# GpSimd in place of SP waits for the last store, and each store has a semaphore of its own

## The chip, the cores and the metric

The kernel runs on one core of a Trainium2 chip. The metric is the device time of one execution in microseconds (us); the median of the runs is given, with the lowest and highest. The core has five engines that run their own instruction streams and meet through semaphores: TensorE (PE), VectorE (DVE), ScalarE (ACT), GpSimd (POOL, or Pool) and SyncE (SP). SP computes nothing; here it issues transfers and waits.

## What is computed

The reference multiplies 16 pairs of matrices, the second one transposed:

```python
batch, m, k, n = 16, 512, 512, 512
a: (batch, m, k) float32
b: (batch, n, k) float32
out = np.matmul(a, b.transpose(0, 2, 1)).astype(np.float32)
```

## The kernel before

**Work and tiles.** The 16 batch elements are taken in 8 pairs. A load brings one input for a whole pair, 2 MB, so there are 16 loads, alternately of `a` and `b`, into the seven slots of `ld`. DVE casts each load to bf16 in two halves of k (`ha`, `wa` for a; `hb`, `wb` for b), PE transposes them in 128x128 blocks into PSUM (`tp`), ACT and DVE copy the results to `ta` and `tb`, PE multiplies them into `ps`, and ACT copies each 512x512 result into one of the seven slots of `ob`. Each result leaves as one store of 1 MB: 16 stores. PE, DVE and ACT run this in loops of the chip over the 8 pairs (L149, L185, L224).

**Who issues and who waits.** The order of the transfers is written out by hand. SP issues all loads (L96) and, between them, tells DVE of each landed load (L116). The string `STORES` (L33) is Pool's list: its eight S are the stores 0 to 7, issued by Pool when ACT has filled the slot (L108, L109); its nine O are waits for the stores 0 to 8 to land, each of which gives a slot of `ob` back to ACT (L135). The stores 8 to 15 are issued by SP, six of them at the places that `LATE` (L36) names and the last two behind all loads. Behind them SP waits for the stores 9 to 14 (L125). Store 15, the last, is waited for in a second critical section (L266, L267). The engines that wait are told apart by `nc.sync` (SP) and `nc.gpsimd` (Pool).

**Semaphores.** A transfer adds 16 to its semaphore when all of it has landed. `landed(n)` (L98) gives the semaphore and the value that stand for store n. Before, Pool's eight stores share five semaphores (`SW = 5`), and a wait for a second store on the same one waits for 32; SP's stores use the semaphores of the load slots, whose count goes on from what the loads have left there:

```python
if n < STORES.count("S"):
    return s_st[n % SW], 16 * (n // SW + 1)
slot = (n - STORES.count("S") + 2) % NL
return s_ld[slot], 16 * (len(range(slot, 2 * pairs, NL)) + 1 + (n - STORES.count("S") >= NL))
```

**The end of the program.** Both critical sections are `tc.tile_critical(no_gpsimd_drain=True)`: with that, the framework puts a NOP on Pool, and a drain on the other engines, behind a section. Between the sections SP collects a signal from each engine (L44). Behind the wait of the second section the engine that waited signals once more (L266). At the end of the whole context, all under L293, every engine has a drain, Pool gathers their signals and releases them, Pool clears the range of semaphores that the program used (EVENT_SEMAPHORE_RANGE_CLEAR), and a second barrier of the same kind closes. In the built program before, Pool's stream behind its L135 waits is: the NOP of L44, the first drain of L293, the gathering of the first barrier, a second drain, the clear, a third drain and the second barrier. SP's is: the signals of L44, a NOP of L266, the waits of L293 (the wait of L267 is among them), a branch, the signal, drain and NOP of L266, and two drains of L293. The cleared range is 99 to 132.

Of the kernel before, what the change touches and what calls it, by code (L numbers as in the profile page):

```python
# [10 lines left out]
def kernel(  # L11
# [6 lines left out]
    nc = tc.nc  # L18
    P = 128
    batch, M, K = a.shape  # L20
# [5 lines left out]
    pairs = batch // 2  # L26
    f32 = mybir.dt.float32
    bf16 = mybir.dt.bfloat16
    NL = 7
# [1 line left out]


    STORES = "SSSSOSOSOSSOOOOOO"  # L33
    SW = 5

    LATE = {11: (8, 9), 13: (10, 11), 15: (12, 13)}  # L36

# [3 lines left out]
    def sem(name):  # L41
        return tc.alloc_semaphore(name)

    with tc.tile_critical(no_gpsimd_drain=True):  # L44
# [11 lines left out]

        s_set = sem("s_set")
        s_ld = [sem(f"s_ld{i}") for i in range(NL)]
        s_st = [sem(f"s_st{i}") for i in range(SW)]

        s_go = sem("s_go")
        s_of = sem("s_of")
# [33 lines left out]
            nc.sync.dma_start(ld[:, slot], src).then_inc(s_ld[slot], 16)  # L96

        def landed(n):  # L98

            if n < STORES.count("S"):  # L100
                return s_st[n % SW], 16 * (n // SW + 1)

            slot = (n - STORES.count("S") + 2) % NL
            return s_ld[slot], 16 * (len(range(slot, 2 * pairs, NL)) + 1 + (n - STORES.count("S") >= NL))

        def store(n):
            engine = nc.gpsimd if n < STORES.count("S") else nc.sync
            engine.wait_ge(s_out, n + 1)  # L108
            engine.dma_start(  # L109
                out[n].rearrange("(p j) n -> p j n", j=J), ob[:, n % NO]  # L110
            ).then_inc(landed(n)[0], 16)

        for n in range(NL):
            load(n)
        for n in range(2 * pairs):
            nc.sync.wait_ge(s_ld[n % NL], 16 * (n // NL + 1)).then_inc(s_go, 1)  # L116

            if n > 0 and n + NL - 1 < 2 * pairs:
                load(n + NL - 1)
            for m in LATE.get(n, ()):  # L120
                store(m)
        store(batch - 2)
        store(batch - 1)
        for n in range(batch - NO, batch - 1):
            nc.sync.wait_ge(*landed(n))  # L125
# [4 lines left out]
        for what in STORES:  # L130
            if what == "S":
                store(n_st)
                n_st += 1
            else:
                nc.gpsimd.wait_ge(*landed(n_of)).then_inc(s_of, 1)  # L135
                n_of += 1
# [127 lines left out]


    with tc.tile_critical(no_gpsimd_drain=True):  # L266
        nc.sync.wait_ge(*landed(batch - 1))  # L267


# [28 lines left out]
```

## Time and profile before

| | us |
|---|---|
| median of 3 runs (lowest, highest) | 125.75 (125.67, 125.76) |
| the profiled execution | 125.76 |
| its span, first to last instruction of the program | 124.0 |
| busy: PE, DVE, ACT, POOL | 92.2, 68.2, 68.1, 5.8 |
| moved in all, mean rate over the span | 50.33 MB, 406 GB/s |
| last store issued by SP (L109) | 114.42 |
| waits of SP at L125 start, first and last | 115.3, 120.2 |
| branch of SP behind the wait for store 15 (L293) | 122.7 |

Times inside the execution count from the start of the span. Busy time is of engine instructions only: semaphore, branch, drain and transfer-issuing instructions belong to an engine's queue and are marked with a q (SPq, POOLq). They are not in the busy figures, but the profile lists them by line with their number, their shortest, median and longest duration in ns, and the first and last start. Line 293 is the launch line at which the context closes; instructions that the framework adds there are recorded under it, even where their wait is written elsewhere.

### The profile page before, as it was taken

The page shows a single profiled execution, that of the slowest core. Times are in us where ns is not written, and L with a number is a line of the kernel's source. Part 1 is how long each engine was busy: PE and PEld are TensorE (multiplying, and loading weights), DVE is VectorE, ACT ScalarE, POOL GpSimd, SP SyncE. Part 2 cuts the span into 40 slices and gives each one's busy share as a digit, 9 for nine tenths or more (in the row PEclk, how much of TensorE's full clock was granted, in tenths as well). Part 3 has the DMA queues.
Part 4 walks back from the last instruction along what each step waited for, and adds up shares of the span by engine and source line. Part 5 has one row for each costly group of instructions (what it writes and reads, how often), then busy time and mean ns, then how long its engine had stood idle before and what let it go on. Part 6 is the DMA issues. An engine that isn't in the chain of part 4 may idle for free. (4 is left out here: it accounts for less than half of the span.)

```text
span 124.0 us, 2364 instructions
## 1 busy us (share of the span) xinstructions
PE 92.2 (74%) x768; PEld 57.5 (46%) x768; DVE 68.2 (55%) x96; ACT 68.1 (55%) x130; POOL 5.8 (5%) x14
## 2 busy tenths in 40 slices
PE   0005099998999899999989998996699909996000
PEld 0005097457547744764476467444554509542000
DVE  0006595948891898389568668913967059400000
ACT  4002415669558946885595679536756085566000
POOL 2000000000000070002020200000000000000000
PEclk9999999999999999999999999999999995999975
DMA  5899999999999999999999999999999999999980
GB/s 100 360 434 444 434 428 423 428 423 423 434 434 434 428 428 407 449 410 441 426 423 441 412 447 428 418 428 428 436 442 410 423 428 426 423 428 426 428 349 11
DMA packets 4608, 50.33 MB, mean 406 GB/s; under 512 B 512, under 2 KB 512, under 8 KB 512
## 3 DMA queue, kind: packets, MB, share of 16 engines
q1 hardware_dynamic: 3456, 41.94, 80.2%
q0 software_dynamic: 1152, 8.39, 16.0%
HBM read 33.55 MB, written 16.78 MB: 406 GB/s over the span
## 5 line engine op out<-in xcount | busy, mean ns | idle before, releaser
L253 PE MATMUL ps<-tb,ta 128*128 128x512 bf16 x256 | 57.7, 379 | 0.4
L211 ACT COPY ob<-ps 128x512 f32 x64 | 34.4, 589 | 29.5 <-PE ps L253 23.2
L193 ACT COPY ta<-tp 128x512 bf16<-128x512 bf16 x64 | 33.0, 610 | 15.7 <-PE tp L234 15.7
L253 PEld LDWEIGHTS ps<-tb,ta 128*128 128x128 bf16 x256 | 24.1, 98 | 30.5 <-issue 3.9
L234 PE MATMUL tp<-ident,ha 128*128 128x128 bf16 x256 | 20.0, 235 | 13.8 <-PEq L139 13.8
L234 PEld LDWEIGHTS tp<-ident,ha 128*128 128x128 bf16 x256 | 17.2, 106 | 17.2 <-issue 15.3
L234 PE MATMUL tp<-ident,hb 128*128 128x128 bf16 x256 | 19.1, 234 | 7.3 <-PEq L139 7.1
L174 DVE COPY tb<-tp 128x1024 bf16<-128x1024 bf16 x32 | 21.2, 684 | 4.8 <-DVEq L139 4.8
L234 PEld LDWEIGHTS tp<-ident,hb 128*128 128x128 bf16 x256 | 17.0, 106 | 8.0 <-issue 8.0
L158 DVE CAST hb<-ld 128x1024 bf16 x8 | 5.5, 688 | 12.7 <-DVEq L139 12.7
L169 DVE COPY ha<-wa 128x2048 bf16<-128x2048 bf16 x8 | 5.5, 690 | 11.4 <-DVEq L139 11.4
L158 DVE CAST ha<-ld 128x1024 bf16 x8 | 5.5, 687 | 10.1 <-DVEq L139 10.0
L164 DVE CAST wa<-ld 128x2048 bf16 x8 | 9.7, 1218 | 0.0
L164 DVE CAST wb<-ld 128x2048 bf16 x8 | 9.7, 1216 | 0.0
L109 POOL DMA_DIRECT2D out_dram<-ob x8 | 5.1, 644 | 64.8 <-DMA ld<-in_b_dram 41.4
L173 DVE COPY hb<-wb 128x2048 bf16<-128x2048 bf16 x8 | 5.5, 685 | 0.2
L161 DVE CAST ha<-ld 128x1024 bf16 x8 | 5.5, 688 | 0.0
L161 DVE CAST hb<-ld 128x1024 bf16 x8 | 5.5, 685 | 0.0
L184 ACT ACT_TABLE_LOAD x1 | 1.3, 1283 | 1.1 <-SPq L44 1.1
L80 POOL TENSOR_SCALAR_AFFINE_SELECT ident<-ident 128x128 bf16<-128x128 bf16 x1 | 0.3, 282 | 0.2 <-POOL ident L78 0.2
L78 POOL MEMSET ident<- 128x128 bf16 x1 | 0.2, 204 | 0.5 <-SPq L44 0.5
L184 ACT COPY one<-const-float32-1.0 128x1 f32<-128x1 f32 x1 | 0.2, 191 | 0.0
(4 smaller groups left out, 0.4 us busy)
## 6 DMA issues: line engine op xcount, KB each, us to landing
ld<-in_a_dram SPq DMA_DIRECT2D x8, 2048.0 KB, 27.8
ld<-in_b_dram SPq DMA_DIRECT2D x8, 2048.0 KB, 30.3
out_dram<-ob POOLq DMA_DIRECT2D x8, 1024.0 KB, 28.7
out_dram<-ob SPq DMA_DIRECT2D x8, 1024.0 KB, 20.4
```

The costliest lines, as they stand in the source:

```text
L109: engine.dma_start(out[n].rearrange("(p j) n -> p j n", j=J), ob[:, n % NO]).then_inc(landed(n)[0], 16)
L158: nc.vector.tensor_copy(out=h[:, :J, :], in_=src[:, :J, :HK]).then_inc(s_cd, 1)
L161: nc.vector.tensor_copy(out=h[:, J:, :], in_=src[:, J:, :HK]).then_inc(s_c, 1)
L164: nc.vector.tensor_copy(out=w[:], in_=src[:, :, HK:]).then_inc(s_w, 1)
L169: nc.vector.tensor_copy(out=ha[:], in_=wa[:]).then_inc(s_ca, 1)
L173: nc.vector.tensor_copy(out=hb[:], in_=wb[:]).then_inc(s_cb, 1)
L174: nc.vector.tensor_copy(out=tb[:, ko, :], in_=tp[:, 2 + ko % 2].rearrange("k j p -> k (j p)"),).then_inc(s_eb, 1)
L184: nc.scalar.copy(out=one[:], in_=nc.const_aps.tensor(1.0, (P, 1), f32))
L193: c = nc.scalar.copy(out=ta[:, ko, e * J * P:(e + 1) * J * P].rearrange("k (j p h) -> k j p h", j=J, h=2), in_=tp[:, ko % 2, :, e * HP:(e ...
L211: c = nc.scalar.copy(out=dst[:, j, :].rearrange("m (p j) -> m p j", j=2 * J), in_=ps[:, j, :].rearrange("m (j p) -> m p j", j=2 * J),)
L234: t = nc.tensor.transpose(tp[:, 2 * x + g, j, :], h[:, j, g * P:(g + 1) * P], ident[:])
L253: t = nc.tensor.matmul(ps[:, j, :], ta[:, ko, (e * J + j) * P:(e * J + j + 1) * P], tb[:, ko, :].rearrange("k (j p) -> k j p", j=2 * J)[:, ...
```

## The change

The wait for store 15 in the second critical section goes from SP to Pool, and each of the 16 stores gets a semaphore of its own, waited for at 16. The helper `landed` becomes one line.

```diff
-    SW = 5
...
-        s_st = [sem(f"s_st{i}") for i in range(SW)]
+        s_st = [sem(f"s_st{i}") for i in range(batch)]
...
         def landed(n):
-            if n < STORES.count("S"):
-                return s_st[n % SW], 16 * (n // SW + 1)
-            slot = (n - STORES.count("S") + 2) % NL
-            return s_ld[slot], 16 * (len(range(slot, 2 * pairs, NL)) + 1 + (n - STORES.count("S") >= NL))
+            return s_st[n], 16

         def store(n):
             engine = nc.gpsimd if n < STORES.count("S") else nc.sync
             engine.wait_ge(s_out, n + 1)
             engine.dma_start(
                 out[n].rearrange("(p j) n -> p j n", j=J), ob[:, n % NO]
-            ).then_inc(landed(n)[0], 16)
+            ).then_inc(s_st[n], 16)
...
     with tc.tile_critical(no_gpsimd_drain=True):
-        nc.sync.wait_ge(*landed(batch - 1))
+        nc.gpsimd.wait_ge(*landed(batch - 1))
```

The kernel's own semaphores go from 28 to 39, and the framework takes one more (a signal of Pool), so that the cleared range becomes 99 to 144. In the built program after, the streams of PE, DVE and ACT are as before but for line numbers, six lower, and so are the issues and waits of SP and Pool up to the end of the first section. The NOP, the waits and the branch, then the signal and the NOPs of the second section now stand on Pool, ahead of its first drain of the closing (L287 is what was L293, L260 what was L266). SP has in their place a wait for Pool's signal, ahead of its two drains.

## The prediction

> **What bounds the kernel now.** I read the page's span and slices first: 124.0 us of span, with the DMA row full until the last two slices, so everything ahead of the last store is set by transfers. Then I cut the end of the span into three stretches with the table by windows (bounds and length in us; busy time of each engine, granted clock, DMA share, GB/s):
>
> ```profile
> 114.00:120.15 6.15, 0.00 (x0) 0.00 (x0) 0.00 (x0) 0.39 (x1) 0.00 (x0) 0.91 1.01 428
> 120.15:122.62 2.47, 0.00 (x0) 0.00 (x0) 0.00 (x0) 0.00 (x0) 0.00 (x0) 0.50 0.09 37
> 122.62:123.95 1.33, 0.00 (x0) 0.00 (x0) 0.00 (x0) 0.00 (x0) 0.00 (x0) 0.50 0.00 0
> ```
>
> Until 120.15 the DMA engines are full with stores, in the next 2.47 us they are nearly done, and in the last 1.33 us nothing moves and no engine works: that is control alone. The queue of SP says what it waited for near the end (total, times, longest):
>
> ```profile
> SPq L125 <- DMA out_dram<-ob: 5.3, 3, 2.4
> SPq L293 <- DMA out_dram<-ob: 1.7, 1, 1.7
> ```
>
> The three waits of L125 take the stores before the last; the 1.7 us at L293 is the wait of L267, recorded under L293, and it ends on the last store, whose last semaphore record stands at 122.62. So the change can touch two things: when 122.62 comes, and the 1.33 us behind it. The instructions of L293, asked by window, show Pool's part there (min/median/max ns, first and last start in us):
>
> ```profile
> L293 POOLq DRAIN  x1: 714/714/714, 120.5 to 120.5; - x1
> ...
> L293 POOLq DRAIN  x1: 113/113/113, 123.3 to 123.3; - x1
> ...
> L293 POOLq EVENT_SEMAPHORE_RANGE_CLEAR  x1: 222/222/222, 123.4 to 123.4; - x1
> ...
> L293 POOLq DRAIN  x1: 34/34/34, 123.7 to 123.7; - x1
> ```
>
> The first row matters most: Pool has nothing left to wait for, so it does its first closing drain, 714 ns, at 120.5, while SP still waits for the last store. It is hidden today with 1.4 us to spare (121.22 to 122.62).
>
> **The change part by part.**
>
> *Eleven more semaphores, each store its own.* In the built order every load, store and wait stands where it stood, on the same engine, and each wait is on the same landing. So the main part costs nothing, covered by a DMA row that is full anyway; 122.62 stays, to within what repeated runs show (125.67 to 125.76, 0.09 us). What grows is the closing clear: semaphores 99 to 132 before (34), 99 to 144 after (46, the framework takes one more for Pool). In the semaphore records the 34 go to zero over 174 ns, in fours 21.7 ns apart. Twelve more are three more fours, +0.065 us. The row itself bounds it above: 222/34 = 6.5 ns each, +0.08; below, 0. The clear stands behind everything, with Pool's last drain after it, so all of it shows. The page "Runtime: NRT & Kernel Launch" of the Trainium skill (The ~15µs preamble/postamble breakdown) gives some 1.5 us for 51 semaphores per engine; by its 29 ns each the term would be an estimated 0.35 us. That is the launch code's own clearing, and no row of this program goes that slowly.
>
> *The wait itself.* SP's closing chain, from the trace, counted from the landing at 122.62: wait over +0.02, branch +0.06, L266 signal +0.215, its drain +0.30, NOP +0.37, two L293 drains +0.42 and +0.48, and Pool's gathering semaphore instruction at +0.513. From there to the end are 0.82 us. After the change Pool walks these steps: wait over +0.03 (its L135 waits end as promptly, 24 ns from landing to start), branch +0.07, signal +0.22, two NOPs +0.31 and +0.38 by SP's spacings, and its drain starts at +0.46 (78 ns after the NOP, as at 120.43 and 120.505).
>
> *The drain that was hidden.* In the built order Pool's first closing drain stands behind the moved wait. Queued behind that wait on Pool are: branch, signal, two NOPs, the drain, the gathering of the barrier, and so every other engine. At 714 ns the drain ends at +1.17, and the gathering instruction starts 44 ns later (the gap after the 186 ns drain at the start), at +1.217 in place of +0.513: +0.704 us. SP's own two drains now wait for Pool's signal (+0.34) and are done near +0.50; they are covered by 0.7 us of Pool's drain and cost nothing. Were that cover gone, the gathering would start near +0.53, +0.02 us against before.
>
> How long will the drain be? The rows are 34, 113, 186 and 714 ns. The short ones follow other work of Pool closely. The long one follows 15 us of pure waiting. A second place shows Pool slow to start when it has sat idle: its stores, whose data had been ready, start late after a wait that has just ended.
>
> ```profile
> L135 POOLq EVENT_SEMAPHORE  x1: 17/17/17, 55.2 to 55.2; - x1
> ```
>
> And from the timeline of Pool (start, length in us):
>
> ```profile
> 43.12 2.49 POOL L109 DMA_DIRECT2D out_dram<-ob  x4 [41.45 <-DMA ld<-in_b_dram]
> 55.78 0.74 POOL L109 DMA_DIRECT2D out_dram<-ob  x1 [10.16 <-DMA out_dram<-ob]
> ```
>
> The wait ends at 55.24 and the store starts 0.54 us later; the others at 63.09 and 70.40 show the same 0.54 to 0.55, while the four of 43.12 run without a gap. So a start after idling costs about half a microsecond, and 714 ns is this with the drain proper (113 to 186): 0.65 to 0.73. After the change the drain has the same history: last store issued long before, then only waits. I take 714 ns, bounds 34 and 750 (the longest Pool row, 748). A gain is excluded by this: no step of SP's chain is shortened, it is only replaced by Pool's equal steps.
>
> Against this speaks the page "VectorE: DVE Perf Modes" (The DRAIN you can't avoid): closing drains are a constant 12 ns or so on all five engines. SP (7), ACT (8), DVE (10) and PE (8) agree here, Pool's four rows do not. By the page the drain would vanish under SP's signals, and the sum would be an estimated 0.09 us.
>
> *Sum.* 0.704 + 0.065 = 0.77 us on the profiled execution's own 125.76 (span 124.0, 1.76 around it, which I leave unchanged): 126.53, with a span of 124.7. The profiled execution is 0.01 above the median, so the forecast of the median is 126.5 us.
>
> **The rivals.**
>
> *The drain is short at its new place (not slower).* The 714 ns would then belong to the moment, for example to the end of the stores, as the DMA share at 120.5 is not yet zero (0.09), and at 123.1 it is. For it: the drains in the quiet are 113 and 34. Against: those two follow another Pool drain within 3 us, and the 0.54 us starts show the lag without a drain. With 113 ns the drain ends at +0.57, the gathering starts at +0.62: 0.10 + 0.065, 125.93 us. It decides from a drain of at most some 180 ns on, where the sum comes to 126.0.
>
> *Pool is slow to wake, and then the drain comes on top.* If the 0.54 us lag sits in Pool's queue and not in the engine behind it, branch and signal start that much later and the drain still takes its 714 ns: 0.77 + 0.54, 127.07 us. Against: at 120.43 Pool's queue went from a 15 us wait to its NOP within 41 ns of SP's signal, and to the drain in 78 ns.
>
> *The edit does not do what it says.* If the main part moved instead (another order of landings, a store earlier), the time would follow 122.62 up or down. The built order shows no such move, and the transfers are the same 50.33 MB; the price is the 0.09 us between runs, or little more.
>
> **How the numbers follow.** What a measurement of this kernel can tell from no change is about 0.2%, 0.25 us: 125.50 to 126.00. The exposed long drain gets 0.78, at 126.53, own range 126.3 to 126.75 (drain of 500 ns to 750, clear of 0 to 0.08, landing 0.09 either way). The short drain gets 0.13, 125.85 to 126.0, no change by the bound. Pool slow to wake, or more, gets 0.06, above 126.75. A moved main part that gains gets 0.03. The range 125.9 to 126.75 takes in the long drain and most of the short one, some 0.88 in all; stopping at 126.0 would leave out more than 2 in 10. Chances: faster 0.03; within 0.2% 0.13; slower 0.78 + 0.06 = 0.84.
>
> **What would show it.** Right: the last store still lands near 122.6; a Pool drain at L287 of about 700 ns that starts some 0.46 us behind that landing; about 2.1 us from landing to end in place of 1.33; a clear of about 287 ns. The forecast is wrong if that drain is under 300 ns, if the landing has moved by more than 0.2 us, or if time is lost between Pool's wait and its drain.

## The result, and the profile after

The changed kernel takes 126.31 us (median of 6 runs, 126.04 to 126.72), beside 125.68 us (125.48 to 125.76) for the kernel before in the same comparison: a ratio of 1.0056, 95% interval 1.0037 to 1.0075. It is slower, by about 0.6 us.

The profiled execution of it took 126.72 us, with a span of 124.9; it is the longest of its six, as that of the kernel before is of the six beside it. A store raises its semaphore in 16 steps, not in one, and "landing" means the last of them. In the kernel before, 15 records of the last store stand from 120.56 to 120.91 us and the sixteenth at 122.62; in the changed one, 15 stand from 120.48 to 121.13 and the sixteenth at 122.80. So in both the end of the transfers hangs on one late part; why it is late was not looked into. The same three stretches of the end, by windows (bounds and length in us; busy time of each engine, granted clock, DMA share, GB/s):

```profile
114.00:120.40 6.40, 0.00 (x0) 0.00 (x0) 0.00 (x0) 0.17 (x1) 0.00 (x0) 0.83 0.98 412
120.40:122.80 2.40, 0.00 (x0) 0.00 (x0) 0.00 (x0) 0.00 (x0) 0.00 (x0) 0.50 0.06 24
122.80:124.92 2.12, 0.00 (x0) 0.00 (x0) 0.00 (x0) 0.00 (x0) 0.00 (x0) 0.50 0.00 0
```

The first two stretches are much as before, with the last landing 0.18 us later. The third, in which nothing moves, has grown from 1.33 to 2.12 us. What SP waits for in its queue has changed hands: behind the stores it now waits for Pool's signal.

```profile
SPq L119 <- DMA out_dram<-ob: 5.7, 3, 2.4
SPq L287 <- POOLq L260: 2.3, 1, 2.3
```

And Pool's instructions of the closing, asked by window (min/median/max ns, first and last start in us):

```profile
L287 POOLq DRAIN  x1: 714/714/714, 123.3 to 123.3; - x1
...
L287 POOLq DRAIN  x1: 130/130/130, 124.2 to 124.2; - x1
...
L287 POOLq EVENT_SEMAPHORE_RANGE_CLEAR  x1: 287/287/287, 124.3 to 124.3; - x1
...
L287 POOLq DRAIN  x1: 34/34/34, 124.7 to 124.7; - x1
```

The 714 ns drain, which stood at 120.5 under SP's wait, now starts at 123.26, 0.460 us behind the landing, and the barrier behind it waits for it. From the landing to Pool's gathering instruction it is 1.218 us in place of 0.513 (+0.705), and from there to the end 0.901 in place of 0.819 (+0.082). That is all of the 0.787 us by which the stretch has grown.

### The profile page after: what moved, and what is told of

The parts are those of the page before. It is cut to its first block, busy times and chain, and to the rows that moved or that the text cites. A ratio compares the mean times of both kernels' runs of the same rounds, so it can differ in the third digit from the quotient of the medians.

```text
span 124.9 us, 2365 instructions
## 1 busy us (share of the span) xinstructions
PE 90.6 (72%) x768; PEld 55.6 (45%) x768; DVE 68.2 (55%) x96; ACT 68.1 (55%) x130; POOL 6.7 (5%) x14
## 5 line engine op out<-in xcount | busy, mean ns | idle before, releaser
L228 PE MATMUL tp<-ident,ha 128*128 128x128 bf16 x256 | 19.3, 230 | 14.6 <-PEq L133 14.6
L228 PEld LDWEIGHTS tp<-ident,ha 128*128 128x128 bf16 x256 | 16.5, 103 | 18.1 <-issue 16.3
L228 PE MATMUL tp<-ident,hb 128*128 128x128 bf16 x256 | 17.8, 225 | 7.7 <-PEq L133 7.4
L228 PEld LDWEIGHTS tp<-ident,hb 128*128 128x128 bf16 x256 | 15.7, 101 | 8.5 <-issue 8.5
L103 POOL DMA_DIRECT2D out_dram<-ob x8 | 6.0, 758 | 64.0 <-DMA ld<-in_b_dram 41.7
```

The source lines that it names most:

```text
L103: engine.dma_start(out[n].rearrange("(p j) n -> p j n", j=J), ob[:, n % NO]).then_inc(s_st[n], 16)
L228: t = nc.tensor.transpose(tp[:, 2 * x + g, j, :], h[:, j, g * P:(g + 1) * P], ident[:])
```

## The experiments

The theory going in was that of the prediction: the hidden drain is the cost, the clear a small part, and the drain is long because Pool has been idle. The table puts together what the profiled executions of all kernels show at their ends; the text below goes through them. Counts are of the transfers that Pool issued and of the semaphores cleared; the rest is in ns. The drain that one kernel adds in the first section is not a closing drain; it is told in the text.

| kernel | Pool's transfers | semaphores | first closing drain of Pool (start, from the last landing) | second drain | clear | last landing to end |
|---|---|---|---|---|---|---|
| before | 8 | 34 | 714 (-2115) | 113 | 222 | 1332 |
| changed | 8 | 46 | 714 (+460) | 130 | 287 | 2119 |
| wait alone | 8 | 35 | 714 (+460) | 119 | 225 | 2046 |
| semaphores alone | 8 | 45 | 714 (-2134) | 129 | 287 | 1412 |
| memset late | 8 | 46 | 714 (+410) | 130 | 288 | 2070 |
| memset early | 8 | 46 | 714 (+460) | 130 | 287 | 2120 |
| a hundred semaphores | 8 | 134 | 714 (-2134) | 258 | 764 | 2020 |
| no store on Pool | 0 | 46 | 41 (+460) | 117 | 288 | 1432 |
| drain in the first section | 8 | 46 | 34 (+458) | 130 | 288 | 1437 |
| four stores on Pool | 4 | 46 | 387 (+460) | 130 | 287 | 1792 |
| halved stores on Pool | 16 | 46 | 1367 (+460) | 130 | 288 | 2774 |

### The change in two halves

The wait alone, on the kernel before:

```diff
-        nc.sync.wait_ge(*landed(batch - 1))
+        nc.gpsimd.wait_ge(*landed(batch - 1))
```

> Only the wait moves to Pool; the stores keep the shared semaphores (cleared range 99 to 133, 35 in place of 34). Theory (the drain that was hidden is the cost): Pool's first closing drain of about 714 ns starts some 0.46 us behind the last landing, the clear is about 227 ns, landing to end about 2.05 us in place of 1.33, and the time is 0.70 us above before. Rival (the semaphores cost more than the clear, for example by moving the landings): then this kernel is less than 0.4 us above before, and the other half, with the semaphores alone, has the rest.

The semaphores alone, on the changed kernel:

```diff
-        nc.gpsimd.wait_ge(*landed(batch - 1))
+        nc.sync.wait_ge(*landed(batch - 1))
```

> Only the semaphores change, one for each store; SP keeps the wait for the last store (cleared range 99 to 143, 45). Theory: the clear grows by eleven at 5.4 ns, to about 282 ns, landing to end 1.39 us, the time 0.06 us above before, less than five rounds can surely tell from nothing. Rival (separate semaphores disturb the transfers): 0.2 us or more above before, with a later last landing and as wide a spread of the runs as the changed kernel showed (126.04 to 126.72).

The wait alone took 126.40 us (126.02 to 126.85), beside 125.49 (125.39 to 125.78) before: 1.0066, interval 1.0047 to 1.0084. The semaphores alone took 125.61 us (125.43 to 125.80): 1.0004, interval 0.9995 to 1.0013, no change that can be measured. The closing instructions of Pool, by line, first with the wait alone, then with the semaphores alone:

```profile
L293 POOLq DRAIN  x3: 34/119/714, 123.0 to 124.3; - x3
L293 POOLq EVENT_SEMAPHORE_RANGE_CLEAR  x1: 225/225/225, 124.1 to 124.1; - x1
```

```profile
L287 POOLq DRAIN  x3: 34/129/714, 120.4 to 123.7; - x3
L287 POOLq EVENT_SEMAPHORE_RANGE_CLEAR  x1: 287/287/287, 123.4 to 123.4; - x1
```

With the wait on Pool the first of the three drains starts at 123.0, behind the landing at 122.54; with the wait on SP it starts at 120.4, ahead of the landing at 122.58. The stretch behind the landing grows by 0.714 us with the wait and by 0.080 with the semaphores; together that is 0.794, beside 0.787 with both. In these stretches the halves add up. In the medians they do so only roughly: the wait alone stands 0.91 us above before, where 0.70 had been expected, and the semaphores alone 0.12, where 0.06 had been. The rival that separate semaphores disturb the transfers falls: that kernel lands at 122.58, and its runs lie as close together as those before (0.37 and 0.39 us).

### Why the drain is long: two memsets

Both give Pool a small piece of work between its last store and the closing drain. Late, in the second section:

```diff
+        warm = sbuf("warm", [P, 1], f32)
...
     with tc.tile_critical(no_gpsimd_drain=True):
+        nc.gpsimd.memset(warm[:], 0.0)
         nc.gpsimd.wait_ge(*landed(batch - 1))
```

> The changed kernel, and Pool writes 128 single numbers into a scratch tile just ahead of its wait for the last store, at about 121 us, in the time in which it would only wait. If the long drain is a start after idling, or the first engine work behind Pool's own transfers, the memset takes that on and the closing drain falls to about 113 to 190 ns: landing to end about 1.5 us and the time 0.55 to 0.6 us below the changed kernel, 0.1 to 0.2 above before. If it is a property of the first closing drain as such, the drain stays near 714 ns and the time at that of the changed kernel.

Early, behind the list of Pool in the first section, with the same tile:

```diff
                 nc.gpsimd.wait_ge(*landed(n_of)).then_inc(s_of, 1)
                 n_of += 1
+        nc.gpsimd.memset(warm[:], 0.0)
```

> As the run with the late memset, but the memset stands at about 105 us, behind Pool's last wait of the first section; then Pool idles for 18 us up to its closing drain. If idling makes the drain long, it is about 714 ns again and the time is that of the changed kernel, 0.6 to 0.75 us above before. If it is the first engine work behind Pool's transfers, whatever the time between, the early memset has taken it on, and the drain is 113 to 190 ns, the time 0.1 to 0.2 us above before.

Neither helps: 126.28 us (126.10 to 126.77) and 126.50 us (126.46 to 126.52), 1.0059 (1.0044 to 1.0074) and 1.0073 (1.0058 to 1.0088). The second is 1.01 us above before, more than the 0.6 to 0.75 expected; its stretch behind the landing is that of the changed kernel (2120 and 2119 ns). The late memset, in the timeline of Pool (start and length in us), and behind it the drains of the same run, by line:

```profile
121.49 0.10 POOL L262 MEMSET warm<- 128x1 f32 x1 [49.09 <-POOLq L261]
```

```profile
L289 POOLq DRAIN  x3: 34/130/714, 123.3 to 124.7; - x3
```

The memset takes 0.10 us and starts 0.19 us behind the start of its branch, the same 0.19 us as the first memset of the program at the branch of 0.76 us, though Pool's engine had been idle for 49.09 us. The early memset, after 33.57 us of idling, starts 0.10 us behind the end of the wait ahead of it. So a memset pays no half microsecond for waking. And 1.7 us after engine work the drain still takes 714 ns. That ends both readings, the start after idling and the first engine work behind the transfers: the time belongs to the drain itself.

### What the drain pays for

Three kernels vary what Pool has issued, and one the place of the first drain. All stores on SP:

```diff
-    LATE = {11: (8, 9), 13: (10, 11), 15: (12, 13)}
+    LATE = {7: (0, 1, 2, 3), 9: (4,), 10: (5,), 11: (6, 7, 8, 9), 13: (10, 11), 15: (12, 13)}
...
-            engine = nc.gpsimd if n < STORES.count("S") else nc.sync
+            engine = nc.sync
...
-        nc.gpsimd.wait_ge(s_ld[0], 32)
         for what in STORES:
-            if what == "S":
-                store(n_st)
-                n_st += 1
-            else:
+            if what == "O":
```

> The changed kernel, with all 16 stores issued by SP: the eight of Pool are put among the loads where SP gets to them (behind load 7 four, behind 9 and 10 one each, behind 11 two). Pool issues no transfer at all; it keeps its nine waits and the wait for the last store, and has been idle since the start. Theory after the memsets (the first closing drain is long because Pool has issued transfers whose bookkeeping it settles there): the drain falls to between 34 and 190 ns. Rival (the first drain on Pool behind the long program is long whatever it issued, for example because its code has to be fetched): 714 ns again. The time itself may move for the other order of stores; with the short drain and the same landing it is 0.1 to 0.2 us above before, with the long one 0.75.

Four stores on Pool, four more on SP:

```diff
-    STORES = "SSSSOSOSOSSOOOOOO"
+    STORES = "SSSSOOOOOOOOO"
-    LATE = {11: (8, 9), 13: (10, 11), 15: (12, 13)}
+    LATE = {9: (4,), 10: (5,), 11: (6, 7, 8, 9), 13: (10, 11), 15: (12, 13)}
```

> The changed kernel with four of Pool's eight stores (4 to 7) given to SP. If the long drain settles the transfers one by one, it is about half, 350 to 450 ns. If it is a fixed price of having issued any, or of the first drain as such, it is 714 ns.

Each store of Pool in two halves:

```diff
-            return s_st[n], 16
+            return s_st[n], 32 if n < STORES.count("S") else 16
...
-            engine.dma_start(
-                out[n].rearrange("(p j) n -> p j n", j=J), ob[:, n % NO]
-            ).then_inc(s_st[n], 16)
+            dst = out[n].rearrange("(p j) n -> p j n", j=J)
+            h = P // 2 if n < STORES.count("S") else P
+            for p in range(0, P, h):
+                engine.dma_start(dst[p:p + h], ob[p:p + h, n % NO]).then_inc(s_st[n], 16)
```

> The changed kernel, with each of Pool's eight stores issued as two of 64 partitions: 16 transfers, the same bytes in the same 8 KB rows. The closing drain stood at 41 ns with no store of Pool's, 387 with four and 714 with eight, about 84 ns each. If the price is for each transfer issued, it is 41 + 16 x 84 = about 1390 ns here, and landing to end about 2.8 us; if it is for the rows or bytes that they moved, it stays at 714.

The drains of Pool by line, with no store, with four stores and with 16 halves on Pool:

```profile
L283 POOLq DRAIN  x3: 34/41/117, 129.8 to 130.5; - x3
```

```profile
L287 POOLq DRAIN  x3: 34/130/387, 126.1 to 127.2; - x3
```

```profile
L288 POOLq DRAIN  x3: 34/130/1367, 126.0 to 128.0; - x3
```

In the first line the first drain is the 41, in the others the longest. 0, 4, 8 and 16 transfers give 41, 387, 714 and 1367 ns: 83 to 87 ns for each transfer (1390 had been expected for 16), and since the halves moved the same bytes in the same rows, the price is for the transfer issued. It does not follow the time that issuing them took either: Pool's eight stores were busy for 5.1 us in the kernel before and for 6.6 with the wait alone, with 714 ns behind both. All of them had landed long before their drain (the last at 105 us in the kernel before, at 111 with the halves). The times of these three kernels are another matter: 132.42, 128.76 and 130.05 us, ratios of 1.0545 (1.0519 to 1.0570), 1.0254 (1.0215 to 1.0293) and 1.0357 (1.0327 to 1.0387). Their last landings stand at 129.37, 125.63 and 125.51, so they lose time in the main part, to the other order or to the splitting of the stores. They were run for the drain, and what exactly delays their stores was not followed up. The time expected of the kernel with no store on Pool, 0.1 to 0.2 us above before, was missed for that reason.

The place of the drain was changed by opening the first section without the option that takes Pool's drain away:

```diff
-    with tc.tile_critical(no_gpsimd_drain=True):
+    with tc.tile_critical():
```

> The changed kernel, with the first critical section opened as tc.tile_critical(), so that the framework puts a drain on Pool in place of the NOP at its end, at about 120.4 us. If the long drain is paid once, by the first drain behind Pool's transfers, it is 714 ns there, hidden as in the kernel before, and the closing drain is 34 to 190 ns: the time 0.1 to 0.2 us above before, 0.55 below the changed kernel. If each such drain takes 714 ns in its place, both are long, and the time is that of the changed kernel.

It took 125.65 us (125.47 to 126.18), beside 125.58 (125.39 to 125.84) before: 1.0005, interval 0.9993 to 1.0017. Pool's drain at the end of the first section, and those of the closing, by line:

```profile
L43 POOLq DRAIN  x1: 714/714/714, 120.4 to 120.4; - x1
```

```profile
L287 POOLq DRAIN  x3: 34/34/130, 123.0 to 123.7; - x3
```

The 714 ns are paid once, at 120.4, while the last store is on its way; the first closing drain is then 34 ns, and the wait on Pool costs next to nothing: SP's two drains now end about when Pool's does. As far as the runs can tell, this recovers the changed kernel's loss. It does not beat the kernel before: its stretch behind the landing is 1437 ns against 1332, and no kernel here points to one that would be measurably faster.

### What the semaphores pay

The kernel before, with names that nothing uses:

```diff
+        for i in range(100):
+            sem(f"s_more{i}")
         s_go = sem("s_go")
```

> The kernel before, with a hundred further semaphores that nothing uses (cleared range 99 to 232, 134 in place of 34). Theory (each name costs only its share of the clear): 100 at 5.4 ns, the clear 222 + 540 = about 765 ns, the time 0.55 us above before. The second closing drain of Pool grew from 113 to 130 ns with 12 more names in the runs so far; if it grows with the names too (1.4 ns each), it is about 250 ns here and the time 0.7 us above before. Rival (the clear is not charged by names): clear under 400 ns, time within 0.15 us of before.

It took 126.23 us (126.14 to 126.49), beside 125.58 (125.39 to 125.84) before: 1.0058, interval 1.0040 to 1.0075. By line:

```profile
L295 POOLq DRAIN  x3: 34/258/714, 120.3 to 124.2; - x3
L295 POOLq EVENT_SEMAPHORE_RANGE_CLEAR  x1: 764/764/764, 123.4 to 123.4; - x1
```

As expected of a price by names: a hundred cost 542 ns in the clear, 5.4 each, and 145 ns in the drain ahead of it, 1.45 each: together 6.9 ns for each name, all of it behind the last landing. The twelve of the change are worth 0.08 us.

## Why the prediction was right, point by point

- **The path and the term.** The forecast of 126.5 us stands beside 126.31. The drain starts 0.460 us behind the landing (forecast 0.46), takes 714 ns (forecast 714), and moves the gathering to +1.218 (forecast +1.217). SP's drains, at +0.40 and +0.46 here, lie under it, as costed.
- **The clear.** 287 ns, as forecast. One small term was missed: the drain ahead of the clear grows with the number of names too, by 17 ns here. So the semaphores were worth 0.082 us, not 0.065, and the whole stretch 0.787, not 0.77.
- **The measured difference** is 0.63 us between the medians, less than the 0.787 by which the stretch behind the landing grew between the two traces; their spans differ by 0.964, the 0.787 and a landing 0.177 later. Every profiled execution with the wait on Pool and eight transfers to settle shows the same 714 ns; what differs is the last landing, between 122.41 and 122.89 us in the profiled executions with eight whole stores on Pool. So the differences of medians, which came out both below and above those of the stretches (0.63 beside 0.787 here, 0.91 beside 0.714 with the wait alone), carry a scatter of some tenths of a us that the prediction did not allow for: its 0.09 us for the landing was too little. The runs of the changed kernel lie further apart (0.68 us) than those before (0.28), and so do those of the wait alone (0.83, beside 0.39); why was not found, and with one trace kept for each kernel it can't be seen whether the landing or the stretch behind it varies there.
- **What was wrong** is the reason given for the length of the drain: "a start after idling costs about half a microsecond". The 714 ns are 34 to 41 ns and some 84 for each of Pool's eight transfers. The 0.54 us between a wait of Pool and its next store, read as the same thing, is not a wake-up of the engine as such: the memsets after 33.57 and 49.09 us of idling show none. What the 0.54 us are, no run here shows. The value was right because the drain's row was taken as it stood, at the same history of transfers, and not because of the reason; to that extent it was luck. With four stores on Pool the same reasoning would have given half a microsecond and the short drain again, and the drain took 387 ns.
- **The rivals.** The short drain did not come: the moment does not set it, the transfers do. Pool slow to wake did not come either: its branch starts 0.074 us behind the landing. The main part did not move: the last landing is 0.18 us later, within the 122.41 to 122.89 of the other traces, and with the semaphores alone it stands at 122.58.
- **The page against the row.** "VectorE: DVE Perf Modes" of the Trainium skill (The DRAIN you can't avoid) has the drains of the launch code, ahead of and behind a kernel, at a constant 12 ns or so on all five engines. The closing drains here are put in by the framework: those of SP, ACT, DVE and PE take 7 to 10 ns in the kernels before and after, Pool's 34 to 1367 over all runs. So the page's figure can't be taken over for Pool's closing drain; the measurement decides. So it does for "Runtime: NRT & Kernel Launch" (The ~15µs preamble/postamble breakdown): an estimated 29 ns for a semaphore by the page, 5.4 in the clear here.

## What to carry to other kernels

Look at what an engine still has to do behind its last wait: here Pool's drain of its own transfers, some 84 ns for each, is free as long as another engine does the last waiting and leaves it the time, and stands bare on the path when Pool waits itself. If Pool has to wait last, let it drain ahead of that wait, while there is something left to wait for. When a row is moved as it stands, its length can be taken over, but the reason for it should be tested before it is used anywhere else.

## What the runs showed of the hardware that was not expected

Pool's first drain behind its transfers takes about 41 ns and 84 for each transfer that it has issued (41, 387, 714, 1367 ns for 0, 4, 8, 16), although they have long landed, and a second drain does not pay again (34 ns). A drain directly ahead of the clear of semaphores grows by 1.45 ns for each semaphore that the clear covers (113 ns at 34, 258 at 134), though it stands before it. Two kernels do not fit: with no store on Pool it was 117 ns at 46, in place of 130, and with the wait alone 119 at 35, where this rate gives about 114. Why it grows, no run here shows.
